# One fixed order for the vector engine at the seams of an attention loop, and another start of the output projection

## The chip, the cores and the metric

The kernel runs on one core of a Trainium2 chip. The core has five engines that run side by side, each with its own in-order instruction queue: TensorE (PE in the profile, with its weight loads as PEld) multiplies matrices, VectorE (DVE) and ScalarE (ACT) work element by element, GpSimd (POOL) does too and issues some DMAs, and SyncE (SP) issues the rest. The metric is the device time of one execution in microseconds (us).

## The reference

The program is a two-layer backbone over 1024 latent positions and a context of 256 positions, 1024 features wide, all in float32. Layer 0 is attention, layer 1 a bidirectional state-space mixer. Each layer is: normalise and modulate, mixer, gated addition to the residual. The change touches layer 0 only. Cut to what matters:

```python
q, k, v, g = split(h @ w_in)                 # 16 query heads, 4 key/value heads of 64
q, k = axial_rope(q), axial_rope(k)          # latent positions only
for each block j of 128 queries:             # 8 latent blocks
    keys = latent blocks j-1, j, j+1 and the 256 context keys
    s = q @ keys.T * scale, masked to |distance| <= 128
    p = softmax over [s, one sink logit per head]
    o = p @ values
y = (o * silu(g)) @ w_out
h = h + gate * y                             # the context is treated likewise
```

## The kernel before

All matrices lie with features on the 128 partitions. To keep float32 accuracy every operand of a product is split into a high part and a low part (`x = h + l`, both in a reduced format), and each product is made of two or three passes: high by high, high by low, low by high.

Attention runs over 40 **units**. A unit is one block of 128 queries and one key/value head, with the four query heads of its group; the units of the context's two blocks come first (`i` = 2, units 0 to 7), then those of latent blocks 0 to 3 (`i` = 0, units 8 to 23), then those of latent blocks 4 to 7 (`i` = 1, units 24 to 39). A unit has `n` key blocks of 128: two for the context, four at the two edges of the latent sequence, five elsewhere.

The loop of `attention` (line 980) goes through a unit's key blocks `k`. For each block it writes down, in this order:

1. `att_turn` (line 793) for block `k + 1`: PE transposes the four heads' probabilities into a PSUM bank `pt`; ACT casts it to the high part `ph` (line 801); DVE subtracts to get the low part `pl` (line 802).
2. `heads`: PE computes the scores of one head of a *later* unit (lines 773 and 774), DVE makes the masked maximum pass over them (line 777, "softmax pass" here), ACT the exponential and its sum (line 779). The scores run a whole unit and one head ahead of their use.
3. parts of a projection (`advance`), which fill PE's time: for `i` = 2 and 0 the gate and query projections of latent blocks 4 to 7 (`qg1`), for `i` = 1 the output projections of the context and of latent blocks 0 to 3 (`out_steps`). A part is a quarter or an eighth of a projection. How many are due is worked out from the key blocks seen so far, `seen[i]`, against all of them, `count[i]`.
4. the two products of block `k` with the values, into the one bank `pv` (line 919 calls them, in `tied`): first with `ph`, then with `pl`.

After a unit's last block, `att_out` (line 813) evacuates `pv`: ACT copies half of it (`co`, line 816), DVE makes two additions (line 819, the last of them kept as `self.added`), POOL multiplies by the gate, and the result is split. Then the first `att_turn` of the next unit is written down. This is what is called a unit's **end** here.

The order of PE's instructions is the written one: `tied` queues each PE instruction behind the one before it. The other engines' orders are chosen by a planner ahead of the run, from the dependences, a model of durations, and a priority that is the written place. `tc.issue_after(x)` adds an edge: what the block writes for the engine of `x` is queued behind `x` on that engine. Instructions written under `high_priority(offset=-300)` count as if written 300 instructions earlier; `advance` does that for the projections, their weight loads, casts and evacuations.

`part` (line 924) runs the projections as generators. The first `next` of one asks for its weights (`load_halves`: two DMAs, two casts, two subtractions), and each later `next` issues one part of its products. The last part is followed by the evacuation: for an output projection the residual addition of line 864 onto a row that a DMA has brought (line 860), for a query projection the rotation (lines 626 to 629). All of these projections share one PSUM bank, `pj`. When the output projections start, at unit 24, the pool of the query projections is closed (`cq.close()`) and its memory is given to the output projections' pool.

Of the kernel before, what the change touches and what calls it, by code (L numbers as in the profile page):

```python
# [111 lines left out]
class Kernel:  # L112
# [13 lines left out]
    def t(self, pool, shape, dt, tag, bufs=None):  # L126
        self.n += 1
        kw = {"bufs": bufs or BUFS.get(tag, 1)}
        return pool.tile(shape, dt, tag=tag, name=f"{tag}_{self.n}", **kw)
# [663 lines left out]
    def att_turn(self, sms, x):  # L793
        nc, t = self.nc, self.t
        pt = t(self.psA, [P, R, P], F32, "pt")
        for r in range(R):
            mm = nc.tensor.transpose(pt[:, r, :], sms[r][:, x * P : (x + 1) * P], self.ident)  # L797
        ph = t(self.pb, [P, R * P], F32R, "ph")
        pl = t(self.pb, [P, R * P], F32R, "pl")
        ptf = pt.rearrange("p r n -> p (r n)")  # L800
        nc.scalar.copy(ph, ptf)  # L801
        nc.vector.tensor_sub(pl, ptf, ph)  # L802
        return mm, (ph, pl)

    def att_gate(self, sg, rs):
# [18 lines left out]
    def attention(self, c0, ckv):  # L824
        nc, t, a = self.nc, self.t, self.a
# [79 lines left out]
        fill = {2: pr[:QC], 0: pr[QC:], 1: out_steps(2) + out_steps(0)}  # L905
# [4 lines left out]
        seen, done = [0, 0, 0], [0, 0, 0]  # L910
        cur = nxt = last = None
        self.pend = []

        def tied(f, *args):
            nonlocal last
            with ExitStack() as c:
                if last:
                    c.enter_context(self.tc.issue_after(last.ins))
                out = f(*args)  # L919
            mm = out[0] if isinstance(out, tuple) else out  # L920
            last = mm or last
            return out
# [16 lines left out]
        def advance(i, m):  # L939
            for _ in range(m):  # L940
                with self.tc.high_priority(offset=-300):
                    tied(part)
                done[i] += 1
                if i == 1 and self.side and done[i] > KT * CPARTS and (done[i] - KT * CPARTS) % SIDE == 0:
                    tied(self.side.pop(0))
# [9 lines left out]
        def last_part(i, d):  # L955
            m = PARTS
            if i == 1:
                m, d = (CPARTS, d) if d < KT * CPARTS else (PARTS, d - KT * CPARTS)
            return d % m == m - 1

        def heads(m):
            for _ in range(m):
                if tied(next, scores, None) is None:
                    break

        def gate(x):
            i, j, b = units[x]
            o = b * P - TT[i][0]
            sg = t(self.psm, [P, 2, P], F32, "sgt")
            nc.sync.dma_start(sg, self.sg_d[j][i][:, :, o : o + P].rearrange("e p n -> p e n"))  # L970
            return sg
# [7 lines left out]
        _, w = tied(self.att_turn, self.pend[0][1], 0)  # L979
        for x, (i, j, b) in enumerate(units):  # L980
            if oH[i] is None:
                if i == 1:
                    i = 0
                    advance(0, total[0] - done[0])
                    i = 1
                    cq.close()
                    self.po = self.pool("op", ctx=c0)
                n = TT[i][1]
                oH[i] = t(self.up, [P, KT, n], F32R, f"uH{i}")
                oL[i] = t(self.up, [P, KT, n], F32R, f"uL{i}")  # L990
            kb, sms, rs = self.pend.pop(0)
            n = len(kb)
            sg1 = gate(x + 1) if x + 1 < len(units) else None
            o = b * P - TT[i][0]
            for k, bb in enumerate(kb):
                if k + 1 < n:
                    _, w1 = tied(self.att_turn, sms, k + 1)
                with ExitStack() as c:
                    if k == 0 and x:
                        c.enter_context(self.tc.issue_after(self.added.ins))  # L1000
                    heads(HEADS_AT[n][k][0])
                seen[i] += 1
                want = min(total[i], -(-total[i] * seen[i] // count[i]) + (k == 0 and n > 2)) - done[i]
                rest, ended = ended and n > 2, False
                m = 0
                while m < want and not rest and not ended:
                    ended = last_part(i, done[i] + m)
                    if ended and n > 2 and k == n - 1:
                        ended = False
                        break  # L1010
                    m += 1
                if k == 0:
                    advance(i, m)
                    pv = t(ps, [P, 512], F32, "pv")
                vv = self.v[:, bb, j, :]
                tied(nc.tensor.matmul, pv, vv, w[0], k == 0, False)
                if k:
                    advance(i, (m + 1) // 2)
                heads(HEADS_AT[n][k][1])
                if k:  # L1020
                    advance(i, m // 2)
                if k == n - 1 and n == 2:
                    tied(self.att_gate, sg, rs)
                tied(nc.tensor.matmul, pv, vv, w[1], False, k == n - 1)
                if k == n - 2 and n > 2:
                    tied(self.att_gate, sg, rs)
                if k == n - 1:
                    self.att_out(pv, sg, oH[i][:, 2 * j : 2 * j + 2, o : o + P], oL[i][:, 2 * j : 2 * j + 2, o : o + P])
                    if self.pend:
                        _, w1 = tied(self.att_turn, self.pend[0][1], 0)  # L1030
                w = w1
            sg = sg1
        advance(1, total[1] - done[1])
# [871 lines left out]
```

## Time and profile before

| | us |
|---|---|
| median of 3 runs | 1800.87 (1799.24 to 1803.06) |
| the profiled execution | 1802.62 |
| its span, first to last instruction | 1800.9 |

| engine | busy us in the span | instructions |
|---|---|---|
| PE | 1742.1 (97%) | 10413 |
| DVE | 1196.9 (66%) | 2119 |
| ACT | 875.4 (49%) | 1902 |
| POOL | 795.4 (44%) | 1066 |

The attention units run from about 255 to 697 us of the span. A timeline row of the profile has the start in us, the duration in us, the engine, the line of the kernel, the operation, what it writes and reads (buffer numbers left out) with shapes, and in brackets how long its engine stood idle before it and which instruction it waited for. Rows with "x2" stand for two instructions in a row. SPq is the queue of DMA issues on SP. A row of the table by stretches has, behind the stretch, its length and the busy time and instruction count of PE, PEld, DVE, ACT and POOL, then the granted clock of PE (1.00 is full speed), the share of time in which the DMA engines were busy, and GB/s. A row of waits has the total in us, the number of times and the longest. PE's rows overlap, since products are pipelined; the distance from start to start is what a product costs there.

### The profile page before, as it was taken

Reading aid. Unit: us, or ns where it says so; the run is one execution under the profiler, and the core shown is the slowest. Engines: PE = TensorE matmul, PEld = TensorE weight load, DVE = VectorE, ACT = ScalarE, POOL = GpSimd, SP = SyncE. Lnnn points to the kernel's source line nnn. Section 1 sums busy time; section 2 is a strip of 40 time slices with the busy share of each in tenths; the row PEclk is TensorE's granted clock in tenths of the full one; section 3 lists DMA queues with packets and bytes.
Section 4 is the critical chain, followed back from the end, with each engine's and each line's share of the span. In section 5 each row is a group of like instructions: output and inputs, shape, how many; then the busy total and the mean of one; then the engine's idle time right before and its main releaser. Section 6 shows DMA issues by size and latency. Waiting matters only on the chain.

```text
span 1800.9 us, 29254 instructions
## 1 busy us (share of the span) xinstructions
PE 1742.1 (97%) x10413; PEld 1506.2 (84%) x10413; DVE 1196.9 (66%) x2119; ACT 875.4 (49%) x1902; POOL 795.4 (44%) x1066
## 2 busy tenths in 40 slices
PE   9999999999989989899999999999999999999997
PEld 6897777887788877679899898989989898988887
DVE  6744346787767765585776767777676777876634
ACT  5522247776667765454343535435353544544522
POOL 3231046555566454202555464645546363554311
PEclk9999999999999999999999999999999999999998
DMA  9478855344444446313323332333333323666533
GB/s 361 167 215 272 271 138 143 91 104 103 112 129 138 107 108 211 102 37 77 76 76 87 71 89 76 86 81 83 82 77 83 93 70 85 174 169 170 174 104 118
DMA packets 211390, 225.54 MB, mean 125 GB/s; under 512 B 15788, under 2 KB 149036, under 8 KB 211244
## 3 DMA queue, kind: packets, MB, share of 16 engines
q1 hardware_dynamic: 177180, 205.02, 38.9%
q0 software_dynamic: 34064, 18.65, 5.5%
q8 instruction: 82, 1.34, 0.3%
q14 instruction: 64, 0.52, 0.1%
HBM read 188.78 MB, written 35.13 MB: 124 GB/s over the span
## 4 chain that ended last, share of the span: by engine, by line
PE 82%; DVE 7%; DMA 4%; ACT 3%; issue 2%; POOL 0%; SPq 0%; DVEq 0%; ACTq 0%; POOLq 0%
PE pj L1302 18%; PE pj L1336 10%; PE pj L1737 7%; PE pj L236 6%; PE pj L237 6%; PE pj L238 6%; PE psD L1287 4%; PE pv L919 3%; PE psX L1489 3%; PE pt L797 3%; PE psD L1405 2%; PE psX L1458 2%; PE psX L1457 2%; DVE sm L777 2%; PE S L773 2%
## 5 line engine op out<-in xcount | busy, mean ns | idle before, releaser
L236 PE MATMUL pj<-uH,wh 128*128 128x512 f32 (+1 forms) x680 | 233.7, 344 | 9.4 <-DVE h L864 3.9
L237 PE MATMUL pj<-uL,wh 128*128 128x512 f32 (+1 forms) x680 | 230.8, 340 | 0.0
L238 PE MATMUL pj<-uH,wl 128*128 128x512 f32 (+1 forms) x680 | 230.2, 339 | 0.0
L1302 PE MATMUL pj<-uH,wh 128*128 128x512 f32 x512 | 173.4, 410 | 1.2 <-ACT bn L1257 1.2
L1302 PE MATMUL pj<-uH,wl 128*128 128x512 f32 x512 | 170.3, 403 | 0.0
L1302 PE MATMUL pj<-uL,wh 128*128 128x512 f32 x512 | 168.3, 402 | 0.0
L1380 POOL TENSOR_TENSOR xw<-xn,dtdec 128x256 f32<-128x256 f32 x144 | 96.2, 669 | 159.7 <-PE psD L1405 75.5
L236 PEld LDWEIGHTS pj<-uH,wh 128*128 128x128 f32 x680 | 130.0, 191 | 33.2 <-DVE qf L667 6.5
L1336 PE MATMUL pj<-wh,uH 128*128 128x256 f32 x512 | 150.8, 295 | 0.0
L1336 PE MATMUL pj<-wl,uH 128*128 128x256 f32 x512 | 150.2, 293 | 0.0
L1336 PE MATMUL pj<-wh,uL 128*128 128x256 f32 x512 | 149.5, 292 | 0.0
L777 DVE CUSTOM_DVE_ANT_0 sm<-S,mask,nsink 128x640 f32<-128x640 f32 (+2 forms) x160 | 123.4, 774 | 38.8 <-PE S L774 37.4
L779 ACT ACTIVATE sm<-sm,nm 128x640 f32<-128x640 f32 (+2 forms) x160 | 119.1, 744 | 51.8 <-DVE nm L777 49.9
L238 PEld LDWEIGHTS pj<-uH,wl 128*128 128x128 f32 x680 | 129.6, 191 | 15.2 <-issue 0.8
L237 PEld LDWEIGHTS pj<-uL,wh 128*128 128x128 f32 x680 | 130.0, 191 | 13.3 <-issue 1.1
L1521 ACT ACTIVATE uT<-psX,nw 128x128 f32<-128x128 f32 x128 | 46.6, 364 | 171.7 <-PE psX L1520 167.7
L802 DVE TENSOR_TENSOR pl<-pt,ph 128x512 fp32r<-128x512 f32 x168 | 113.7, 685 | 21.6 <-ACT ph L801 21.0
L221 POOL TENSOR_TENSOR wl<-wr,wh 128x512 fp32r<-128x512 f32 x74 | 97.0, 1314 | 67.9 <-ACT wh L219 64.3
L219 ACT CAST wh<-wr 128x512 fp32r<-128x512 f32 (+1 forms) x116 | 75.0, 649 | 92.3 <-PE pj L237 68.0
L1302 PEld LDWEIGHTS pj<-uH,wl 128*128 128x128 f32 x512 | 95.7, 188 | 19.9
L801 ACT CAST ph<-pt 128x512 fp32r<-128x512 f32 x168 | 95.2, 584 | 35.0 <-PE pt L797 26.8
L1302 PEld LDWEIGHTS pj<-uL,wh 128*128 128x128 f32 x512 | 95.3, 188 | 19.3
(352 smaller groups left out, 4940.4 us busy)
## 6 DMA issues: line engine op xcount, KB each, us to landing
wr<-w_x SPq DMA_DIRECT2D x32, 512.0 KB, 3.9
M<-acs SPq DMA_DIRECT2D x64, 256.0 KB, 5.1
bw<-acs SPq DMA_DIRECT2D x64, 256.0 KB, 5.5
wr<-w_sk SPq DMA_DIRECT2D x24, 512.0 KB, 4.2
wr<-wg SPq DMA_DIRECT2D x40, 256.0 KB, 5.0
qs<-q POOLq DMA_DIRECT2D x40, 256.0 KB, 3.7
wada<-w_ada SPq DMA_DIRECT2D x16, 512.0 KB, 8.9
wr<-wq SPq DMA_DIRECT2D x32, 256.0 KB, 3.0
```

The source lines that it names most:

```text
L221: (eng or nc.vector).tensor_tensor(l, raw, h, op=ALU.subtract)
L236: self.nc.tensor.matmul(ps, lh, rh, start=first and i == 0, stop=False)
L237: self.nc.tensor.matmul(ps, lh, rl, start=False, stop=False)
L238: self.last_mm = self.nc.tensor.matmul(ps, ll, rh, start=False, stop=last and i == n - 1)
L777: nc.vector.tensor_tensor_reduce(out=sm[:, :W], in0=Sv, in1=self.mask[:, m0 : m0 + W], scale=-SCALE, scalar=self.nsink[:, 4 * j + r : 4 * ...
L779: nc.scalar.activation(sm[:, :W], sm[:, :W], AF.Exp, bias=nm[:, r : r + 1], scale=-1.0, accum_out=sums[:, r : r + 1])
L801: nc.scalar.copy(ph, ptf)
L802: nc.vector.tensor_sub(pl, ptf, ph)
L1302: self.pe = nc.tensor.matmul(raw[:, 512 * i : 512 * i + 512], l[:, k, :], r[i][:, k, :], start=k + y == 0, stop=k == KT - 1 and y == 2)
L1336: self.pe = nc.tensor.matmul(pj[:, c], l, r[:, k, :], start=c % 2 + q + k + y == 0, stop=c % 2 == 1 and q == 1 and k == 3 and y == 2)
L1380: nc.gpsimd.tensor_tensor(xw, X(st, c).rearrange("p (r h) -> p r h", r=R), self.dtdec[:, c, hd(d, g)].unsqueeze(2).broadcast_to([P, R, HP] ...
L1737: self.pe = nc.tensor.matmul(banks[x], l[:, z, sl], r, start=k == 2 * qs[0] and y == 0, stop=k == 2 * qs[-1] + 1 and y == 2)
```

## The change

Three things are changed, all in the order of work; no instruction is added or taken away.

- At a unit's end, the low part of the next unit's first block is queued behind the unit's last output addition on DVE (`issue_after(self.added.ins)` around `att_turn`).
- In a unit's first block, the head that is scored there has its DVE instructions queued behind that low part, where they were queued behind the output addition. `att_turn` keeps its last low part in `self.lowered` for this, and the loop reads it before it writes the next `att_turn`.
- When the units of latent blocks 4 to 7 begin, the first output projection's generator is started at once, so that its weights are asked for there, in plain written order, and not with the first part that is due. `seen[1]` then starts at -3, so parts become due three key blocks later than before, and some are left for the `advance` behind the last unit.

```diff
@@ att_turn
-        nc.vector.tensor_sub(pl, ptf, ph)
+        self.lowered = nc.vector.tensor_sub(pl, ptf, ph)
@@ attention, at the first unit of latent blocks 4 to 7
                     cq.close()
                     self.po = self.pool("op", ctx=c0)
+                    cur = fill[1].pop(0)()
+                    next(cur)
+                    seen[1] = -3
@@ attention, the loop over key blocks
             for k, bb in enumerate(kb):
+                low = self.lowered
                 if k + 1 < n:
                     _, w1 = tied(self.att_turn, sms, k + 1)
                 with ExitStack() as c:
                     if k == 0 and x:
-                        c.enter_context(self.tc.issue_after(self.added.ins))
+                        c.enter_context(self.tc.issue_after(low.ins))
                     heads(HEADS_AT[n][k][0])
@@ attention, a unit's end
                     if self.pend:
-                        _, w1 = tied(self.att_turn, self.pend[0][1], 0)
+                        with self.tc.issue_after(self.added.ins):
+                            _, w1 = tied(self.att_turn, self.pend[0][1], 0)
```

## The prediction

> **What bounds the kernel now.** I read the page first, then the busy table by stretches, then TensorE's waits inside the attention, then the timeline at single places.
>
> ```profile
> PE 1742.1 (97%) x10413; PEld 1506.2 (84%) x10413; DVE 1196.9 (66%) x2119; ACT 875.4 (49%) x1902; POOL 795.4 (44%) x1066
> 312.00:497.00 185.00, 174.20 (x1008) 147.50 (x1008) 142.78 (x310) 130.01 (x286) 97.69 (x143) 1.00 0.43 103
> 510.00:515.00 5.00, 3.37 (x16) 3.37 (x17) 0.57 (x2) 1.03 (x2) 0.40 (x1) 0.53 0.57 145
> PE pv L919 <- DVE pl L802: 19.4, 27, 2.5
> ```
>
> The first row is the page's: TensorE (PE) is the bound over the whole program, so only time in which PE stands still can be won, and nothing in the change shortens PE's own work. The second row is the stretch of the units of latent blocks 0 to 3 (185 us): PE is busy 174.20, VectorE (DVE) 142.78 and ScalarE (ACT) 130.01, so DVE has slack on average, and what PE loses there are short waits. The fourth row is the largest of PE's waits between 250 and 700 us: the second product of a key block (pv from pl, line 919) waits for the low part (line 802), 27 times, 19.4 us in all. I sorted these 27 by their place in the timeline: 18 of them, 15.5 us, are the first low part after a unit's end. The first of the 18 (with the product ahead of it) and the last are the three upper rows here; the next two are an end of the other order, the last row a wait that is not at an end.
>
> ```profile
> 312.82 0.47 PE L919 MATMUL pv<-ph,v 128*128 128x512 f32 x1 [1.39 <-DVE ot L819]
> 314.12 0.50 PE L919 MATMUL pv<-pl,v 128*128 128x512 f32 x1 [0.83 <-DVE pl L802]
> 681.02 0.50 PE L919 MATMUL pv<-pl,v 128*128 128x512 f32 x1 [0.84 <-DVE pl L802]
> 642.74 0.47 PE L919 MATMUL pv<-ph,v 128*128 128x512 f32 x1 [0.43 <-DVE ot L819]
> 643.38 0.50 PE L919 MATMUL pv<-pl,v 128*128 128x512 f32 x1 [0.17 <-DVE pl L802]
> 414.49 0.51 PE L919 MATMUL pv<-pl,v 128*128 128x512 f32 x1 [0.89 <-DVE pl L802]
> ```
>
> One such end from the timeline, unit 11 to 12 (columns: start, duration, engine, line, operation):
>
> ```profile
> 351.88 0.58 ACT L816 COPY co<-pv 64x512 f32<-64x512 f32 x1
> ...
> 352.49 1.08 ACT L801 CAST ph<-pt 128x512 fp32r<-128x512 f32 x2
> 352.50 0.85 DVE L819 TENSOR_TENSOR ot<-pv,co 64x256 f32<-64x256 f32 x2 [1.51 <-ACT co L816]
> ...
> 353.37 0.88 DVE L777 CUSTOM_DVE_ANT_0 sm<-S,mask,nsink 128x640 f32<-128x640 f32 x1
> ...
> 353.79 0.40 PE L919 MATMUL pv<-ph,v 128*128 128x512 f32 x1
> ...
> 354.18 1.28 DVE L802 TENSOR_TENSOR pl<-pt,ph 128x512 fp32r<-128x512 f32 x2
> ...
> 354.92 0.50 PE L919 MATMUL pv<-pl,v 128*128 128x512 f32 x1 [0.74 <-DVE pl L802]
> ```
>
> ACT copies the half of pv (co), then casts the next unit's high part. DVE makes the two additions until 353.35, then a softmax pass of a head that is needed a whole unit later (line 777, until about 354.2), and only then the two low parts. PE's first product starts at 353.79, its second at 354.92: 1.13 us from start to start. Now an end at which DVE happened to take the low part first:
>
> ```profile
> 410.23 0.85 DVE L819 TENSOR_TENSOR ot<-pv,co 64x256 f32<-64x256 f32 x2 [0.18 <-ACT co L816]
> ...
> 411.11 0.69 DVE L802 TENSOR_TENSOR pl<-pt,ph 128x512 fp32r<-128x512 f32 x1
> ...
> 411.57 0.40 PE L919 MATMUL pv<-ph,v 128*128 128x512 f32 x1
> 411.72 0.88 DVE L777 CUSTOM_DVE_ANT_0 sm<-S,mask,nsink 128x640 f32<-128x640 f32 x1
> 411.86 0.50 PE L919 MATMUL pv<-pl,v 128*128 128x512 f32 x1
> ```
>
> Additions until 411.08, low part, softmax; the two products are 0.29 us apart. DVE does the same work in both; only the order differs. I went through the 38 ends: the low part is behind the additions at all of them, ahead of the softmax at 14, behind it at 24.
>
> **The change part by part.**
>
> *The order on DVE.* The edge from the additions to the low part changes nothing by itself (that order holds at 38 of 38). The edge from the low part to the softmax turns round the 24. Nothing is added to any engine. Per end there are two prices. Where PE comes to its first product some 0.4 us after the additions, 1.13 falls to 0.29: 0.84 us. Where PE itself stands waiting for the additions, the first product starts 0.15 us after them, and the rows at 642.74 and 643.38 give 0.64 from start to start, where the rows at 312.82 and 314.12 have 1.30 (and others up to 1.4): 0.7 us. Of the 18 waits, 9 are of the first kind (three a little shorter: 9 x 0.84 - 0.3 = 7.3 us), 7 of the second (7 x 0.73 = 5.1 us), one is worth 0.3, and one is this:
>
> ```profile
> 667.41 1.39 DVE L297 SCALAR_TENSOR_TENSOR h<-h,mod,ut 128x256 f32<-128x256 f32 x1 [0.62 <-DMA h<-h]
> ...
> 669.52 0.51 PE L919 MATMUL pv<-pl,v 128*128 128x512 f32 x1 [2.54 <-DVE pl L802]
> ```
>
> There a modulation of the context stream (line 297), itself waiting for its DMA, sits on DVE between the softmax and the low part. The edges do not name it; it may land in front of the low part or behind it. Bounds 0.9 and 2.7 us, I take 1.3. Sum 14.0 us.
>
> What is late next: the second key block's low part (pl1). It is worth counting, because in unit 16, where the order is already the new one, PE lost 0.89 us at 414.49 on exactly that: two rotation passes of a query projection stood on DVE ahead of it. On the plain end, softmax plus both low parts end as late as now (355.46 for unit 11), and PE, which takes 1.49 us for a block (rows below), would use pl1 at 354.92 + 1.49 - 0.84 = 355.57: no wait. Six of the 18 ends lie where query rotations run on DVE; I take half of 0.8 us back there (2.4), and 0.1 at each of the other twelve (1.1). Bounds for this: 0 and the whole 14.0. Gain of the order: 10.5 us.
>
> The added edge makes the softmax wait. Behind it on DVE stand the next low parts and any evacuation of a projection; for its result wait only ACT's exponential and the score bank, which is asked for again two heads later. If the low part is late, all of these are; that is the third rival below.
>
> *Weights asked for sooner, and the pace.* The loads of the first output weights move, in written order, ahead of the unit; they lose the priority that the others of this kind have. I cost that at nothing: a load of output weights (wo) is already issued at 488.79 on the queue of SyncE (SP), ten us before the first product on them at 498.54, and after the change that product comes later still. If this cover were gone, a load of 3 to 4 us would stand open once.
>
> ```profile
> 488.79 0.54 SPq L229 DMA_DIRECT2D wr<-wo  x1
> ...
> 506.81 0.33 SPq L229 DMA_DIRECT2D wr<-wo  x1
> 507.19 2.11 SPq L860 DMA_DIRECT2D h<-ctxT  x2
> ```
> ```profile
> 498.54 0.39 PE L236 MATMUL pj<-uH,wh 128*128 128x256 f32 x1 [1.37 <-DVE rope_b L627]
> ...
> 511.63 0.58 PE L236 MATMUL pj<-uH,wh 128*128 128x256 f32 x1 [3.94 <-DVE h L864]
> 512.01 0.41 PE L237 MATMUL pj<-uL,wh 128*128 128x256 f32 x1
> 512.22 0.41 PE L238 MATMUL pj<-uH,wl 128*128 128x256 f32 x1
> ```
> ```profile
> 495.66 0.85 DVE L819 TENSOR_TENSOR ot<-pv,co 64x256 f32<-64x256 f32 x2 [0.19 <-ACT co L816]
> ...
> 511.09 0.48 DVE L864 SCALAR_TENSOR_TENSOR h<-pj,mod,h 128x256 f32<-128x256 f32 x1 [2.70 <-DMA h<-ctxT]
> ...
> 516.92 0.85 DVE L819 TENSOR_TENSOR ot<-pv,co 64x256 f32<-64x256 f32 x2 [5.26 <-ACT co L816]
> ```
>
> The gain here is from the count that starts at -3: in unit 24 the first output projection starts at the fourth key block in place of the first, and its second one (m = 1) in unit 25 in place of unit 24's last block. PE now loses 1.37 us at 498.54 (the one projection bank is still read by the last query rotation) and 3.94 at 511.63: the second projection needs the bank, which the residual (line 864) frees, which waits for the context rows, whose DMA stood on SP behind a weight load at 506.81 and landed 3.9 us after its issue. Then the clock: the window row 510 to 515 shows 0.53, and 18 products start 0.21 us apart, of which 0.47 x 0.21 x 18 = 1.8 us are lost. Together 7.1 us. The projection now ends at the head of unit 25, about 510 by unit 24's length, and the next use of the bank is two blocks later, past 511.1: I count all 7.1 as removed. Against it: three blocks of unit 24 have no projection under them. A block without one takes PE 1.49 us:
>
> ```profile
> 488.30 0.60 PE L797 MATMUL pt<-ident,sm 128*128 128x128 f32 x4
> ...
> 489.79 0.60 PE L797 MATMUL pt<-ident,sm 128*128 128x128 f32 x4
> ```
>
> DVE needs 0.69 + 0.88 there for its low part and softmax, 0.1 more than PE, and has the rotation of the last query projection besides; the wait at 414.49, behind two passes of such a rotation, was 0.89, and the rotation has four. So some 2.0 us. Bounds 0 and 4. Gain 5.1 us, bounds 3 and 7.
>
> About four projection parts slip behind the last unit. They are PE work in both versions and run back to back there. Behind them comes the normalisation of latent block 0 to 3, whose end has room:
>
> ```profile
> 734.06 0.74 DVE L299 SCALAR_TENSOR_TENSOR uL<-h,mod,uH 128x512 fp32r<-128x512 f32 x1
> ...
> 744.99 0.69 DVE L872 TENSOR_TENSOR sqa<-sqa,ut 128x512 f32<-128x512 f32 x1 [0.76 <-ACT ut L871]
> ```
>
> The last modulation ends at 734.8 and the other half's last square at 745.7; four parts of three products, at 0.40 us or less each, are under 5 us. Nothing.
>
> *Sum.* 10.5 + 5.1 = 15.6 us. The profiled execution took 1802.6 us, so 1787.0; the median of the runs is 1.7 us lower, and the forecast stands against it: 1800.9 - 15.6 = **1785 us**.
>
> **The rivals.**
>
> *The wait moves on.* pl1 takes pl0's place at most ends, as in unit 16. For it: rotations and residuals are on DVE in most units. Against it: of the 14 ends of the new order only unit 16 shows it in full, and the nine waits that are not at an end make 3.9 us together. The ends then bring 5 us: 1800.9 - 5 - 5.1 = 1791.
>
> *The clock falls in unit 24.* PE has no projection for three blocks; a large part of what is left are transposes and waits. If the clock went to half for these blocks, 3 x 1.49 us are added: 1789. Against it: the granted clock is 1.00 over the stretch 312 to 497, which has blocks like that in each unit. [...]
>
> *Slower: the softmax is held by a late high part.* Today DVE does the softmax while ACT is still behind with the cast (line 801); afterwards DVE stands, and PE with it.
>
> ```profile
> 354.51 0.83 ACT L779 ACTIVATE sm<-sm,nm 128x640 f32<-128x640 f32 x1
> ```
> ```profile
> DVE pl L802 <- ACT ph L801: 21.0, 19, 2.8
> ```
>
> At the shown end the first of the two casts is done at about 353.05, 0.3 us before the additions. With an exponential (0.83) and another cast (half of 1.08) ahead of it, it ends 1.1 behind them. At some 21 ends PE comes to the first product within 0.6 us of the additions and would lose that: 21 x 1.1 = 23 us, where now 14.0 are lost: 9 slower, less the 5.1 of the other part: 1805. It decides from 19.1 / 21 = 0.9 us of lateness on. For it: DVE's low parts already wait for casts, 19 times, 21.0 us (second row). Against it: no edge touches ACT, and those waits are mostly within units, where the cast is on time for PE.
>
> *No change.* The same lateness at 0.9 us: the ends lose what they win and the other part goes with it, 1801. Only the loads' being asked for sooner is a part that I expect to do nothing, as above.
>
> **How the numbers follow.** Forecast 0.62; the wait moves on 0.20; the clock 0.05; held softmax 0.09; nothing 0.04. A measurement of this kernel tells about 0.2% (3.6 us) from no change: faster by more 0.87, within 0.04, slower 0.09. The lower end takes the upper bounds: ends 14.0 + 1.4 (the row at 669.52) and 7.1, and 1.5 for small waits of the context units, 24 us, 1777. The upper end takes in the moved wait with its transition at the lower bound of 3 and a little of its own spread: 1795.
>
> **What would show it.** In the changed profile: TensorE's wait of pv for pl between 250 and 700 us falls from 19.4 to 8 or less; at the ends the order additions, low part, softmax, and 0.3 or 0.64 us between the first two products; no 3.9 us wait for line 864 and no granted clock near 0.5 between 500 and 520; unit 24 is shorter by 5 us and more than it is now (from the additions at 495.66 to those at 516.92), and four projection parts stand behind the last unit. It is wrong if a wait for pl1, or for line 801 on DVE, takes up the difference, or if the 21 us of unit 24 stay.

## The result, and the profile after

The changed kernel takes 1782.87 us (median of 3 runs, 1782.51 to 1784.75), against 1800.87 before: 18.0 us less, a ratio of 0.9902 with a 95% interval of [0.9879, 0.9924]. The forecast was 1785, in a range of 1777 to 1795. The profiled execution of the changed kernel took 1782.51 us and spans 1780.8.

The lines of the page and of the table by stretches that answer to those of before:

```profile
PE 1737.2 (98%) x10413; PEld 1503.8 (84%) x10413; DVE 1194.3 (67%) x2119; ACT 874.6 (49%) x1902; POOL 795.0 (45%) x1066
```
```profile
312.00:497.00 185.00, 180.05 (x1049) 153.13 (x1050) 149.32 (x324) 135.71 (x299) 101.16 (x148) 1.00 0.43 105
497.00:518.00 21.00, 20.62 (x150) 18.90 (x149) 14.82 (x34) 15.83 (x35) 15.57 (x21) 1.00 0.68 176
```

The instruction counts of all engines are the same, and PE's busy time is nearly so. What changed is how the work is packed: in the same 185 us PE is busy 180.05 in place of 174.20. In the stretch in which unit 24 begins, the granted clock is 1.00 throughout; before, it was 0.53 in 510 to 515. Three of PE's waits between 250 and 700 us in the changed kernel (total, times, longest); the one left out, for line 667, has 2.9 us (3.8 before):

```profile
PE pv L919 <- DVE pl L802: 7.0, 18, 1.3
PE pv L919 <- DVE ot L819: 3.1, 5, 1.4
PE pv L919 <- ACT ph L801: 2.7, 1, 2.7
```

The wait for the low part fell from 19.4 to 7.0 us, and the 3.9 us wait for line 864 is gone. A wait of 2.7 us for a high part is new; the experiment `mods` is about it. It is not the same in every execution: in a second one of this kernel (`after_again`, below) the longest of its kind is 1.2 us.

The same end as in the prediction, unit 11 to 12, from the timeline of the changed kernel, and below it the end of the other kind that before stood at 312.82 and 314.12:

```profile
349.73 1.08 ACT L801 CAST ph<-pt 128x512 fp32r<-128x512 f32 x2
349.73 0.85 DVE L819 TENSOR_TENSOR ot<-pv,co 64x256 f32<-64x256 f32 x2 [1.51 <-ACT co L816]
350.61 0.69 DVE L802 TENSOR_TENSOR pl<-pt,ph 128x512 fp32r<-128x512 f32 x1
...
351.03 0.40 PE L919 MATMUL pv<-ph,v 128*128 128x512 f32 x1
351.22 0.88 DVE L777 CUSTOM_DVE_ANT_0 sm<-S,mask,nsink 128x640 f32<-128x640 f32 x1
...
351.36 0.50 PE L919 MATMUL pv<-pl,v 128*128 128x512 f32 x1
```
```profile
312.21 0.47 PE L919 MATMUL pv<-ph,v 128*128 128x512 f32 x1 [1.40 <-DVE ot L819]
...
312.84 0.51 PE L919 MATMUL pv<-pl,v 128*128 128x512 f32 x1 [0.16 <-DVE pl L802]
```

Additions, low part, softmax pass: the order that the edges ask for, at all 38 ends. Before, the trace has the low part behind the softmax at 23 of them, one fewer than the prediction counted. The two products start 0.33 us apart (before 1.13) and 0.63 us apart (before 1.30).

To see where the time came from, I cut each profiled span at the ends of the last output additions (line 819) of units 0, 23, 24 and 37, and subtracted:

| us | to unit 0's end | units 1 to 23 | unit 24 | units 25 to 37 | the rest | span |
|---|---|---|---|---|---|---|
| before | 260.2 | 236.3 | 21.3 | 161.8 | 1121.3 | 1800.9 |
| after | 259.5 | 229.7 | 12.0 | 159.0 | 1120.6 | 1780.8 |
| after, second execution | 258.7 | 231.4 | 12.0 | 157.5 | 1123.5 | 1783.0 |
| `no_early` | 259.5 | 229.8 | 12.0 | 159.3 | 1122.0 | 1782.5 |
| `order_only` | 259.2 | 231.3 | 22.2 | 158.1 | 1121.5 | 1792.3 |
| `start_only` | 260.9 | 237.6 | 12.0 | 158.2 | 1121.1 | 1789.8 |
| `no_pace` | 259.8 | 231.4 | 19.5 | 158.0 | 1120.3 | 1788.9 |
| `mods` | 259.6 | 229.8 | 12.0 | 154.4 | 1120.8 | 1776.5 |
| `evac_low` | 258.4 | 227.1 | 12.0 | 158.1 | 1122.7 | 1778.4 |
| `both` | 259.5 | 227.1 | 12.0 | 151.5 | 1120.8 | 1770.9 |
| `pace6` | 260.3 | 229.7 | 10.1 | 153.6 | 1137.0 | 1790.8 |

Between the first two lines, units 1 to 23 gave 6.6 us, unit 24 gave 9.3, units 25 to 37 gave 2.8. The two executions of the changed kernel, and `no_early`, whose instructions stand in the same order, show what one figure of the table is worth: up to 1.8 us of a long stretch, and 3 us of the rest, are spread; unit 24 takes 12.0 us in all three. The 1.7 us in units 1 to 23 have a likely cause in the trace: in the second execution the granted clock is 0.50 for 3.4 us from 312.6 on (rows in the last section), and half of 3.4, an estimate of what that costs, is 1.7. `order_only`, `start_only` and `no_pace` have such a stretch at the same unit, the other kernels of the table have none there. In units 25 to 37 the kernel before, the changed kernel's first execution, `no_early` and `evac_low` have one each.

### The profile page after: what moved, and what is told of

Its sections match the earlier page's. It is cut to its first block, busy times and chain, and to the rows that moved or that the text cites. A ratio compares the mean times of both kernels' runs of the same rounds, so it can differ in the third digit from the quotient of the medians.

```text
span 1780.8 us, 29267 instructions
## 1 busy us (share of the span) xinstructions
PE 1737.2 (98%) x10413; PEld 1503.8 (84%) x10413; DVE 1194.3 (67%) x2119; ACT 874.6 (49%) x1902; POOL 795.0 (45%) x1066
## 4 chain that ended last, share of the span: by engine, by line
PE 84%; DVE 8%; issue 3%; ACT 3%; DMA 2%; POOL 0%; SPq 0%; DVEq 0%; ACTq 0%; POOLq 0%
PE pj L1307 18%; PE pj L1341 10%; PE pj L1742 7%; PE pj L236 6%; PE pj L237 6%; PE pj L238 6%; PE psD L1292 4%; PE pv L919 3%; PE psX L1494 3%; PE pt L797 3%; PE psD L1410 2%; PE S L773 2%; PE psX L1463 2%; PE psX L1462 2%; DMA h<-h 1%
## 5 line engine op out<-in xcount | busy, mean ns | idle before, releaser
L238 PE MATMUL pj<-uH,wl 128*128 128x512 f32 (+1 forms) x680 | 229.7, 339 | 0.0
L236 PEld LDWEIGHTS pj<-uH,wh 128*128 128x128 f32 x680 | 129.0, 190 | 28.1 <-DVE qf L667 6.6
L1307 PEld LDWEIGHTS pj<-uH,wh 128*128 128x128 f32 x512 | 93.4, 189 | 17.9 <-ACT bn L1262 1.4
```

Of the source, the lines that this page charges most:

```text
L236: self.nc.tensor.matmul(ps, lh, rh, start=first and i == 0, stop=False)
L238: self.last_mm = self.nc.tensor.matmul(ps, ll, rh, start=False, stop=last and i == n - 1)
L1307: self.pe = nc.tensor.matmul(raw[:, 512 * i : 512 * i + 512], l[:, k, :], r[i][:, k, :], start=k + y == 0, stop=k == KT - 1 and y == 2)
```

## The experiments

All were timed against the kernel before on the same chip. Ratios are to the kernel before.

### The parts of the change, one by one

`order_only`: the two edges, without the three lines at the start of latent blocks 4 to 7.

```diff
-                    cur = fill[1].pop(0)()
-                    next(cur)
-                    seen[1] = -3
```

> The two edges on DVE alone; the output projections start as before. Theory (the ends are worth 10.5 us, the start of the output projections the rest): about 1790 us; PE's wait of pv for pl between 250 and 700 us near 7 to 9 us in place of 19.4; the stop of 3.9 us before line 864 and the low clock after it stay. Rival (the wait moves on to the next low part): 1796, with the same order at the ends but a wait for pl of 14 us or more.

Measured: 1792.27 us (1789.55 to 1794.27) beside 1800.52, ratio 0.9952 [0.9935, 0.9969]. PE's waits and the window in which unit 24's projections stand:

```profile
PE pv L919 <- DVE pl L802: 9.5, 21, 1.6
PE pj L236 <- DVE h L864: 4.8, 1, 4.8
```
```profile
505.00:510.00 5.00, 3.44 (x16) 3.45 (x17) 0.57 (x2) 1.03 (x2) 0.40 (x1) 0.50 0.40 107
```

The order alone takes 9.9 us off the waits for the low part and 8.3 us off the median. Unit 24 keeps its wait for line 864, now 4.8 us, and its half clock (0.50). The wait that stood at 669.52 before is still there, and a modulation that waits for its DMA is still ahead of the low part:

```profile
661.18 0.48 DVE L297 SCALAR_TENSOR_TENSOR h<-h,mod,ut 128x256 f32<-128x256 f32 x1 [1.97 <-DMA h<-h]
...
662.32 0.51 PE L919 MATMUL pv<-pl,v 128*128 128x512 f32 x1 [1.65 <-DVE pl L802]
```

`start_only`: the start of the output projections without the two edges.

```diff
-                        c.enter_context(self.tc.issue_after(low.ins))
+                        c.enter_context(self.tc.issue_after(self.added.ins))
...
-                        with self.tc.issue_after(self.added.ins):
-                            _, w1 = tied(self.att_turn, self.pend[0][1], 0)
+                        _, w1 = tied(self.att_turn, self.pend[0][1], 0)
```

> The other start of the output projections alone (weights asked for ahead of the unit, count from -3); the order on DVE as before. Theory: unit 24 goes from 21.3 us to about 12, of which some 2.7 us are four projection parts that only move, so 1794 us; PE's wait of pv for pl stays near 19 us. Rival (the start pays only where the order keeps the uncovered blocks of unit 24 free of waits): 1798 or more, with new waits of 3 us in unit 24.

Measured: 1791.93 us (1790.11 to 1793.69), ratio 0.9951 [0.9933, 0.9969].

```profile
PE pv L919 <- DVE pl L802: 15.4, 25, 1.0
```

Of the waits for the low part 15.4 of 19.4 us stay, fewer than expected, and the list has no wait for line 864. The table shows the gain where it should be: unit 24 takes 12.0 us. Units 25 to 37 are 3.6 us shorter too, and there the longest wait for a low part is now 1.0 us: the 2.54 us stop at 669.52 of the kernel before is not there, and with it most of the 4.0 us.

The two parts add up: 0.9952 x 0.9951 = 0.9903, and the whole has 0.9902 here and 0.9909 [0.9889, 0.9930] in a second measurement (`after_again`, below). As far as these intervals tell, neither hides the other.

Of the two edges, only the second does anything. Neither was timed alone, but `start_only`, which has neither, has the low part behind the additions at all 38 ends, so the first edge has nothing to turn round. In the programs as the planner orders them it is the same: with the edge from the additions to the low part alone, the instructions of every engine stand in the same order as in `start_only`; with the edge from the low part to the softmax alone, in the same order as in the changed kernel.

`no_pace`: the first output projection is still started at once, but `seen[1]` counts from 0.

```diff
-                    seen[1] = -3
```

> The changed kernel without the count's start at -3: the weights are still asked for ahead of the unit, but parts are due from unit 24's first block as before. Theory (asking sooner brings nothing, the pace brings all of the start): the same as the two edges alone, about 1790, with the stop of some 4 us before line 864 in unit 24. Rival (asking sooner removes the stop): 1783 to 1785, without the stop.

Measured: 1791.23 us (1789.14 to 1792.68), ratio 0.9946 [0.9931, 0.9962]: in time not to be told from `order_only`.

```profile
504.98 0.39 PE L236 MATMUL pj<-uH,wh 128*128 128x256 f32 x1 [2.65 <-DVE h L864]
```
```profile
505.00:510.00 5.00, 5.00 (x28) 4.88 (x29) 0.22 (x2) 1.79 (x4) 1.68 (x2) 0.66 0.56 126
```

The wait for line 864 is there again, 2.65 us where `order_only` has 4.8, and unit 24 takes 19.5 us where that one has 22.2. This is no effect of the early start: in the two traces every engine, and the DMA queue, runs the same instructions in the same order. The 2.65 and 4.8 us are two executions of one order, and show how far this wait spreads; in the kernel before, line 864 waited for the DMA of the context's row (2.70 us, to 511.09). So the early start does nothing here. What removes the stop is the count from -3.

`no_early`: the reverse, the count from -3 without the early start.

```diff
-                    cur = fill[1].pop(0)()
-                    next(cur)
```

> The changed kernel without the early request of the weights, but with the count from -3. Its instructions stand in the same order as the changed kernel's on every engine, the DMA queues with them, so the theory (asking sooner brings nothing) expects 1783 within 0.2%, and the distance is a reading of the measurement's own spread. Rival: none that the order of instructions leaves.

Measured: 1786.57 us (1784.25 to 1789.98), ratio 0.9923 [0.9902, 0.9943]. Its instructions stand in the same order as the changed kernel's on every engine, and unit 24 takes 12.0 us in both. The 3.7 us between the medians are therefore no effect of the edit. The intervals overlap, and the difference shows what two sets of runs of one order can be apart. With the count at -3 too, asking for the weights sooner does nothing.

### The rival with the late cast

In the prediction, the slower case was a softmax held by a late high part, with a threshold of 0.9 us of lateness. To make the cast late, ACT casts the bank twice more at every unit's end before the cast that is used.

```diff
-    def att_turn(self, sms, x):
+    def att_turn(self, sms, x, first=False):
...
+        for _ in range(2 if first else 0):
+            nc.scalar.copy(ph, ptf)
         nc.scalar.copy(ph, ptf)
```

`late_old` has this with the old order on DVE (and the new start of the output projections), so it stands to `start_only` as `late_new`, which has it in the changed kernel, stands to the changed kernel. (The planner then puts the softmax first at all 38 ends of `late_old`, where `start_only` has it first at 24.) Line numbers behind the edit are two higher.

> The other start of the output projections with the order on DVE as before, and two needless repeats of the cast to the high part ahead of the one that counts, at each of 39 unit ends: the high part then comes about 1.1 us later. Theory: the softmax pass fills the time on DVE while the cast is late, so part of the lateness is hidden; 1791 without the repeats becomes about 1805. Rival (the softmax hides nothing, every end pays the whole 1.1 us where PE comes early): 1815.

> The changed kernel with the same two needless repeats of the cast at each unit end. Theory (the third rival of the prediction: with a late high part the softmax is held, and the order's gain is gone from about 0.9 us of lateness on): within 4 us of the kernel with the old order and the same repeats, so about 1805. Rival (the order's gain stays whatever the cast does): 8 us under it.

Measured: `late_old` 1863.03 us (1861.94 to 1867.22), ratio 1.0340 [1.0321, 1.0359]; `late_new` 1857.0 us (1851.19 to 1860.16), ratio 1.0305 [1.0280, 1.0329]. The largest of PE's waits between 250 and 700 us in each, the old order first, and below it the rows of one end from its timeline:

```profile
PE pv L921 <- ACT ph L803: 44.4, 30, 3.4
```
```profile
346.87 0.85 DVE L821 TENSOR_TENSOR ot<-pv,co 64x256 f32<-64x256 f32 x2
...
347.75 0.75 DVE L777 CUSTOM_DVE_ANT_0 sm<-S,mask,nsink 128x512 f32<-128x512 f32 x1
...
350.12 0.60 ACT L803 CAST ph<-pt 128x512 fp32r<-128x512 f32 x1
350.75 1.29 DVE L804 TENSOR_TENSOR pl<-pt,ph 128x512 fp32r<-128x512 f32 x2 [2.15 <-ACT ph L803]
...
350.77 0.49 PE L921 MATMUL pv<-ph,v 128*128 128x512 f32 x1 [0.69 <-ACT ph L803]
...
351.50 0.51 PE L921 MATMUL pv<-pl,v 128*128 128x512 f32 x1 [0.23 <-DVE pl L804]
```
```profile
PE pv L921 <- ACT ph L803: 41.2, 29, 3.8
```
```profile
347.04 1.29 DVE L804 TENSOR_TENSOR pl<-pt,ph 128x512 fp32r<-128x512 f32 x2 [2.13 <-ACT ph L803]
347.06 0.49 PE L921 MATMUL pv<-ph,v 128*128 128x512 f32 x1
...
347.79 0.51 PE L921 MATMUL pv<-pl,v 128*128 128x512 f32 x1 [0.23 <-DVE pl L804]
348.25 0.74 DVE L777 CUSTOM_DVE_ANT_0 sm<-S,mask,nsink 128x512 f32<-128x512 f32 x1
```

At the shown end of the old order the cast ends at 350.72, 3.0 us behind the additions (347.72): far past the threshold. Over the 38 ends it comes 1.3 to 3.9 us behind them. The price, some 70 us in both kernels, is far above what I expected. The casts stand in ACT's queue between its other work, so two of 0.6 us make the last one later by more than 1.2, and PE itself, which needs the high part for the first product, waits for it 41 to 44 us.

But the new order stays 6.0 us ahead of the old one (medians; the ratios differ by 0.0035, and each is known to about 0.002). Without the late cast `start_only` and the changed kernel differ by 0.0042 to 0.0049 of the time before, 7.6 to 8.8 us. The rows show one half of it. In both orders the low part starts 0.03 us after the cast, and the products are 0.73 us apart; the old order has the softmax done in the hole before, the new one does it in the hole behind. As PE waits for the cast either way, the held softmax costs nothing at these two products, but by these rows the new order should gain nothing there either.

What it gains comes in part by way of ACT's queue, which the prediction looked at for the kernel before alone: in the old order the exponential of the softmax pass gets onto ACT between the additions and the last cast at 21 of the 38 ends, in the new one at 2, and the cast comes 2.3 us behind the additions on average in the old order and 2.0 in the new. From 255 to 745 us PE waits 51.6 us for the high part in the old order and 45.0 in the new. The held softmax is not free: in the new order PE waits 3.5 us, in 7 places, for a softmax pass (line 777) before it can write scores, and the list of the old one has no such wait. A further part is the clock: the profiled execution of the old order has 65 us at half clock ahead of its last 10 us, that of the new one 51 (mean granted clock 0.981 and 0.984).

So at 1.3 to 3.9 us of lateness the rival, with its threshold of 0.9, does not come true: the new order is not the slower one. Between 0.9 and 1.3 us no run tests it.

### What the left-over waits are

`mods`: the 2.7 us wait for a high part. In the timeline of the changed kernel:

```profile
591.89 6.39 SPq L890 DMA_DIRECT2D h<-h  x2
...
596.39 0.48 DVE L297 SCALAR_TENSOR_TENSOR h<-h,mod,ut 128x256 f32<-128x256 f32 x1 [4.59 <-DMA h<-h]
596.91 0.51 ACT L298 ACTIVATE uH<-h,mod 128x256 fp32r<-128x256 f32 x1 [4.76 <-DVE h L297]
...
598.55 0.50 PE L919 MATMUL pv<-ph,v 128*128 128x512 f32 x1 [2.69 <-ACT ph L801]
```

A modulation of the context stream (line 297) stands at the head of DVE's queue and waits 4.59 us for its row. ACT waits for DVE (4.76 us), and the cast that PE needs stands behind that. The kernel asks for each row only when its modulation is written. In `mods` the rows are asked for in pairs, one pair ahead, in the memory of a tile that is free then:

```diff
                 self.alloc_u(i)
+                if i == 2:
+                    rows(0)
                 return self.spread_mm
+            def rows(k):
+                st["rows"] = t(self.po, [P, 2, n], F32, "dg0")
+                for x in range(2):
+                    nc.sync.dma_start(st["rows"][:, x], self.h_d[k + x][i])
...
+                elif i == 2:
+                    h = st["rows"][:, k % 2]
                 else:
...
                 self.modulate(1, h, st["r"], i, k)
+                if i == 2 and k % 2 and k < KT - 1:
+                    rows(k + 1)
```

> The changed kernel, with the rows for the context's modulations asked for two at a time and ahead of their use, in a tile of their own. Theory (the two longest waits left, 2.7 us for a cast and 1.1 us for the additions, come from a modulation on DVE that waits for its row): both go, 1783 becomes 1779. Rival (they are hidden or come back at another place): 1783.

Measured: 1778.67 us (1778.20 to 1779.01), ratio 0.9873 [0.9858, 0.9888]. Units 25 to 37 take 154.4 us where the changed kernel takes 159.0 in one execution and 157.5 in the other; the other stretches are within 0.2 us of the first of them. The largest of PE's waits (line 919 is 930 here):

```profile
PE pv L930 <- DVE pl L802: 9.0, 17, 1.3
```

No wait for a high part is left in the list. The waits for the low part are 2.0 us more than in the changed kernel, so a part of what was won came back there.

`evac_low`: most of the 7.0 us for the low part. The longest in the changed kernel:

```profile
396.60 1.74 DVE L648 TENSOR_TENSOR ql<-qf,qh 128x512 fp32r<-128x512 f32 x1
...
397.29 0.39 PE L919 MATMUL pv<-ph,v 128*128 128x512 f32 x1
398.25 0.68 DVE L802 TENSOR_TENSOR pl<-pt,ph 128x512 fp32r<-128x512 f32 x1
...
398.99 0.50 PE L919 MATMUL pv<-pl,v 128*128 128x512 f32 x1 [1.30 <-DVE pl L802]
```

This is the low part of a unit's second block, and it stands behind the splitting of a rotated query (line 648, 1.74 us). `evac_low` adds one more edge: what a projection part writes for DVE is queued behind the last low part that is written.

```diff
-                    tied(part)
+                    with ExitStack() as c:
+                        if hasattr(self, "lowered"):
+                            c.enter_context(self.tc.issue_after(self.lowered.ins))
+                        tied(part)
```

> The changed kernel, with the DVE instructions of the projections' evacuations queued behind the last low part written before them. Theory (the waits of 0.9 to 1.3 us within units 14 to 22 come from rotation passes ahead of a low part): PE's wait of pv for pl falls from 7.0 to about 3 us, 1779. Rival (the projection bank comes free later and PE waits for it in place of the low part): 1783 to 1790, with waits for lines 627, 667 or 864.

Measured: 1781.16 us (1779.73 to 1785.66), ratio 0.9892 [0.9871, 0.9912]: not to be told from the changed kernel in time. The trace shows the effect, but a small one:

```profile
PE pv L919 <- DVE pl L802: 5.1, 14, 1.3
PE pv L919 <- DVE ot L819: 4.3, 5, 2.2
```

1.9 us less for the low part, 1.2 us more for the additions; a 1.28 us wait behind line 648 is still there at 397.86. Units 1 to 23 take 227.1 us, here and again in `both`, where the changed kernel takes 229.7 without a stretch at half clock.

`after_again`, `both` and `pace6` ran on one chip. `after_again` is the changed kernel, once more.

> The changed kernel once more, as the measure for the two beside it: 1783 to 1787, ratio 0.990 to 0.992 to the kernel before. If the ends and the start add up (0.9952 and 0.9951 alone), 0.9903.

Measured: 1785.09 us (1782.66 to 1788.96) beside 1801.73, ratio 0.9909 [0.9889, 0.9930].

`both` is `mods` and `evac_low` together.

> The changed kernel with the context rows asked for ahead in a tile of their own and the evacuations' DVE instructions queued behind the last low part. Theory (two separate waits): 4 and 2 us under the changed kernel, 1777. Rival (evacuations held back meet the rows' modulations on DVE, and the second brings nothing beside the first): the same as the rows alone, 1779.

Measured: **1773.82 us** (1771.57 to 1777.17), ratio 0.9848 [0.9825, 0.9871]. It beats both kernels, the changed one on the same chip by 11.3 us.

```profile
PE pv L930 <- DVE pl L802: 4.3, 11, 1.3
```

Units 25 to 37 fall to 151.5 us, 2.9 us below `mods`, while `evac_low` alone took only 0.9 us off them; its trace has a stretch at half clock there, which that of `both` has not. Whether the two edits together give more than their sum is not shown: the product of their ratios over that of the changed kernel is 0.9856 to 0.9863, and this lies in the interval of `both`.

### How far the start can be put off

`pace6`: the count from -6.

```diff
-                    seen[1] = -3
+                    seen[1] = -6
```

> The changed kernel with the count starting at -6 in place of -3. Theory (the pace pays because the second output projection no longer needs the bank before the context row is there; once it is past that, more delay brings nothing, and unit 24 has fewer parts under its short waits): 0 to 3 us slower than with -3. Rival (each part moved behind the last unit is worth time by itself): 2 us faster.

Measured: 1792.23 us (1790.75 to 1795.96), ratio 0.9951 [0.9932, 0.9969]: 7.1 us behind the changed kernel on the same chip. The units themselves are shorter again (unit 24 by 1.9 us, units 25 to 37 by 4 to 5). The rest is 16.4 us longer than in the changed kernel's first profile, 13.5 than in the second. From its timeline, the first and the longest of the stops behind the last unit, and the stretch with the longest, then the same stretch of the changed kernel:

```profile
727.28 0.50 PE L236 MATMUL pj<-uH,wdth 128*128 128x512 f32 x1 [3.44 <-ACT cacc L1126]
...
785.03 1.97 PE L1261 MATMUL pj<-ident,bT 128*128 128x128 f32 x8 [7.96 <-DVE bT L1219]
```
```profile
780.00:800.00 20.00, 14.29 (x68) 11.98 (x68) 12.80 (x16) 10.92 (x23) 1.04 (x1) 0.66 0.48 110
```
```profile
780.00:800.00 20.00, 18.86 (x105) 16.22 (x104) 17.19 (x23) 11.85 (x28) 0.00 (x0) 1.00 0.24 61
```

With three more blocks of projections behind the last unit, the normalisation comes too late for layer 1's start: PE stops four times for 2.2 to 8.0 us (at 736.90 and 740.13 too), and the granted clock is 0.66 over 780 to 800. The changed kernel has one stop there, of 3.65 us at 730.74.

## Why the prediction was right

**The order (10.5 us).** Measured alone: 8.3 us between the medians, and the interval of its ratio, 5.6 to 11.7 us, holds 10.5. By its own steps: the ends were turned round (23 by the trace, not 24), the edge from the additions did nothing, and the two prices per end, 1.13 to 0.29 and 1.30 to 0.64, came out as 1.13 to 0.33 and 1.30 to 0.63. At the 38 ends, 15.7 us of waits for the low part became 3.2 in `order_only`, 12.5 less where the sum has 14.0. The row at 669.52, for which I had bounds of 0.9 and 2.7, gave the lower one: 1.65 us of it is left in `order_only`, for the order of softmax and low part was not its cause; it is the DMA that DVE waits for. With the other start it went, and in the changed kernel a stop of the same kind appeared at 598.55, at another modulation and now on the high part.

**What is late next (3.5 us back).** In `order_only` the waits for the low part away from the ends grew from 3.9 to 6.6 us: 2.7 back. The bound that I set for the whole, a remaining wait for the low part of 8 or less, held in the changed kernel with 7.0. The longest of what is left, the 1.30 us at 398.99, is on the low part of a second block behind the work on a query, as in unit 16 before.

**The start (5.1 us, bounds 3 to 7).** Measured alone: 8.6 us, interval 5.6 to 12.1. This is the term that was too small, in two of its parts. Both stops went, 1.37 and 3.94 us, as counted. The half clock was worth more than the 1.8 us that I put: in the kernel before it lasts from 510.3 to 517.1 (0.50), PE is at work for 5.5 us of this, and half of that, an estimate, is 2.7. And what I set against it was 2.0 us of new waits in the blocks of unit 24 that have no projection. The trace of the changed kernel shows two such waits, and then the first projection part:

```profile
490.63 0.50 PE L919 MATMUL pv<-pl,v 128*128 128x512 f32 x1 [0.47 <-DVE pl L802]
...
492.67 0.50 PE L919 MATMUL pv<-pl,v 128*128 128x512 f32 x1 [0.28 <-DVE pl L802]
...
495.23 0.28 PE L236 MATMUL pj<-uH,wh 128*128 128x256 f32 x1
495.35 0.28 PE L237 MATMUL pj<-uL,wh 128*128 128x256 f32 x1
```

0.75 us in place of 2.0. So the parts make 1.37 + 3.94 + 2.7 - 0.75 = 7.3 us. Unit 24 fell by 9.3 us; 18 of the projections' products have left it (42 in it before, 24 after, counted in the records), worth 2.2 us at the 0.12 us from start to start of these rows, but that work only moves. The two together are 9.5. The stop at 669.52 is a second source for the 8.6: `start_only` lost it too (units 25 to 37 shorter by 3.6 us). In the whole change that gain was not had beside the order's: these units gave 2.8 us there, where each half alone gave 3.6 or 3.7.

So the sum was 15.6 and the measured difference 18.0, with the order's term somewhat below its forecast and the start's above it. That the median came within about 2 us of the forecast is in part luck: the two terms erred by 2.2 and 3.5 us in opposite directions.

**Weights sooner: nothing.** Right: with it or without it the instructions stand in the same order, at either start of the count (`no_early`, `no_pace`).

**The parts behind the last unit: nothing.** Right for the count of -3, within the 3 us by which the rest spreads: it took 1120.6 to 1123.5 us against 1121.3. Behind the last product of the attention the records have 6 to 8 products of projections and before none, two to three parts in place of the four that I named. `pace6` shows that the room has an end: with six blocks it is used up.

**The rivals.** The moved wait did not come. Its trace would have been 14 or more of waits for the low part. The clock stayed at 1.00 from 497 to 518, and in the blocks of unit 24 without a projection ahead of that: the changed kernel has no half clock between 316 and 599 in either execution. The held softmax did not come either, and with a cast made late the new order was still not the slower one. I had overlooked that PE needs the cast itself, so a late cast stops the first product in both orders.

## What to carry to other kernels

Where a bound engine waits a little at every seam of a loop, look at what stands ahead of the awaited instruction in the other engine's queue: turning round two of them adds no work and here gave 0.7 to 0.8 us at a seam where the bound engine waited. A modulation that waited for its DMA at the head of DVE's queue held what stood behind it, on other engines too (DVE stood for 4.59 us, ACT for 4.76 and PE for 2.69 at 598.55 of the changed kernel); asking for its data a step sooner was worth some 3 to 5 us here in the stretch that it touches. Work that is put off costs nothing only as far as there is room behind: three blocks were free, and six cost 7 us against three.

## What was unexpected of the hardware

The granted clock fell after shorter stops than the 3.94 us of the kernel before: after 2.65 us in `no_pace` (rows above), after 2.54 us at 669.52 in the kernel before (0.66 over 670 to 675), after 2.69 us at 598.55 in the changed kernel (0.50 over 599.2 to 602.6). It also fell after the stop of 1.40 us at the start of unit 8 in four traces, and did not after the same stop in seven others, nor after one of 2.71 us in `late_new`. Two executions of the changed kernel differ in this. The stretches of 3.4 us ahead of the fall and behind it, first at 598.55, then at unit 8 in the second execution, then the first stretch at unit 8 in the first execution, where the clock stayed at 1.00:

```profile
595.80:599.20 3.40, 0.71 (x4) 0.56 (x4) 1.64 (x4) 1.59 (x4) 1.20 (x1) 1.00 0.05 9
599.20:602.60 3.40, 3.40 (x15) 3.00 (x14) 2.88 (x9) 1.90 (x4) 0.63 (x3) 0.50 0.38 107
```
```profile
309.20:312.60 3.40, 1.84 (x12) 1.28 (x11) 2.74 (x7) 2.67 (x7) 1.65 (x4) 1.00 0.60 184
312.60:316.00 3.40, 3.40 (x13) 2.91 (x12) 2.04 (x5) 2.10 (x5) 1.04 (x2) 0.50 0.14 39
```
```profile
309.10:312.50 3.40, 2.00 (x15) 1.54 (x13) 2.34 (x5) 3.24 (x8) 1.64 (x2) 1.00 0.81 196
```

In each of the 13 traces the places at which the granted clock changes lie whole multiples of 3.413 us apart. In the kernel before it changes at 510.25, 517.08, 670.68, 674.09, 749.19 and 756.01, which is 2, 45, 1, 22 and 2 times 3.413 us from one to the next; in the changed kernel at 599.20, 602.61, 732.32 and 735.73, which is 1, 38 and 1 times. Where these steps lie differs from execution to execution: counted back by them, one comes at 312.28 in the kernel before and one at 312.48 in the changed kernel, and the stop at unit 8 ends at 312.82 and at 312.21.

Cut along these steps between 255 and 700 us, the traces come near to showing what goes with a fall: all 23 stretches in which PE stood still for 56% or more were followed by one at half clock, of the 1615 stretches at full clock with 40% or less none was, and of the 29 between them 10 were. (The ends of products are modelled, so these shares are rough.) In the kernel before, the stretches with 75% (from 506.84) and 66% (from 667.27) were followed by half clock, and the one with 40% from 312.28 on was not; in the changed kernel, the one with 79% (from 595.78) was, and the one with 41% (from 309.06) was not. PE did not stand still for the whole of a stretch ahead of a fall: in the rows it was at work for 0.71 us from 595.80 on and for 1.84 us from 309.20 on. So in these traces the share of a stretch that PE stood still tells the falls apart better than the length of the stop does: the 1.40 us at unit 8 came with a fall and without one.

A stretch of 3.4 us at half clock in which PE is the bound costs, as an estimate, 1.7 us, half of 3.4, besides the stop: in the kernel before, products of 128x512 start 0.43 us apart from 671.27 to 672.55, where the clock is 0.50, and 0.23 us apart from 674.42 on, where it is 1.00. Units 1 to 23 differ by as much between two executions of one kernel (229.7 and 231.4 us).
